# Ring tiles of 768 instead of 770 columns, and a first block whose convolution reads no history

## The chip, the cores and the metric

The kernel runs on one core of one Trainium2 chip. The metric is device time in microseconds, the median of several executions; before the change it was 2507.09 us in three (2506.99 to 2508.43).

## What is computed

One layer of a hybrid model is applied to 2048 prompt tokens and to 64 tokens of a sample that continues an earlier sequence. All arithmetic is float32; the widths are 1024 (model), 8 heads of 128 (path B) and 256 (side input).

```python
proj = rms_norm(x, g_pre) @ w_in                 # 1024 -> 10 x 1024
vA, bA, cA, zA, q, f, iv, zB, gA, gB = split(proj)
u = cA * vA
u_ext = concat([conv_hist, u])                   # two tokens of history; zeros for the prompt
conv = w[0] * u_ext[0:T] + w[1] * u_ext[1:T+1] + w[2] * u_ext[2:T+2]
yA = (silu(zA) * bA * conv) @ w_a_out
new_conv = u_ext[-2:]
# path B: gated recurrence over chunks of 64 tokens, o normalised per head
yB = (o * silu(zB)) @ w_b_out
out = (sigmoid(gA) * yA + sigmoid(gB) * yB) @ w_o
x = x + rms_norm(out, g_post)
x = x + (p @ w_ple_proj) * sigmoid(rms_norm(x, g_ple) @ w_ple_gate)
```

The outputs are x for prompt and sample, the last two columns of u for both, and the final states of path B for both.

## The kernel before

Everything is held with features on the 128 partitions and tokens along the columns. The 2112 tokens stand in one row (1408 of the prompt, the 64 of the sample, the other 640 of the prompt) and are cut into three blocks of 768, 704 and 640 columns, done one after the other. Within a block a matrix product takes halves of 384, 352 or 320 columns as its moving operand.

A float32 product is made of three matmuls in a reduced format: each operand is split into a high part (a copy by ACT) and the remainder (a subtraction by DVE, both in `split`, L230), and TensorE (PE) adds hi by hi, hi by lo and lo by hi into the same PSUM bank. In `sgroup` (L457 to L459), `in_turn` (L608 to L610) and `mm3` (L645 to L647) these three are the innermost lines. `sgroup` and `in_turn` do a 2x2 block product with seven instead of eight partial products, from sums of weight blocks and sums of operand halves. The plain products of the side input are L1313 to L1315.

Weights come by DMA in tiles of 128x512, issued by SyncE's queue, into a pool of their own (`raw`, `hi`, `lo`, `s`). Almost everything else on chip lies in one ring of 48 tiles: operands, activations, gates, intermediate rows. `rt()` (L155) hands out the next tile of that ring, `[P, BN + 2]` float32, of which callers use the first 768, 704 or 640 columns. BN is 768; the two extra columns are there for one use, the convolution's u, which needs two columns of history ahead of each run of tokens.

In SBUF each tile is given a multiple of 32 bytes per partition. The weight tiles of 2048 bytes all start at a multiple of 64. A ring tile of 770 columns is 3080 bytes and takes 3104; the ring starts at byte 70080, which is a multiple of 64.

The order of instructions on an engine is the order in which the program is written, with priorities (`tc.high_priority`) and places (`issue_after`, `hooks`) that put side work between the matmuls. DVE, ACT and POOL each run their rows in order; POOL also issues the DMAs of ring tiles, SyncE those of weights.

The change touches `path_a`, the stage of each block after path B, which runs over eight column groups j. For each j: POOL copies two columns of history ahead of each run of tokens in u (L899: from `hist_p` for the prompt, from `hist_s` for the sample); `sgroup` makes vA and cA, whose product DVE writes into u behind the history (`times_u`, L906); ACT multiplies u by the first tap into `conv` (L923), DVE adds the two others (L925, twice), and POOL copies u's last two columns back into the history (L926). Then zA and bA are made and multiplied in. `hist_p` is set to zero at the start (L195); block 0 has a single run, all of the prompt. Blocks 1 and 2 have two runs and one.

Of the kernel before, what the change touches and what calls it, by code (L numbers as in the profile page):

```python
# [14 lines left out]
ALU = mybir.AluOpType  # L15
# [3 lines left out]
P = 128  # L19
# [18 lines left out]
BN = max(SIZES)  # L38
# [56 lines left out]
def hybrid_step(  # L95
# [17 lines left out]
    V, A, G, T, SP = nc.vector, nc.scalar, nc.gpsimd, nc.tensor, nc.sync  # L113
# [5 lines left out]
    ring = ctx.enter_context(tc.tile_pool(name="ring", bufs=RING))  # L119
# [7 lines left out]
    def nm(s):  # L127
        uid[0] += 1
        return f"{s}_{uid[0]}"
# [22 lines left out]
    def hn():  # L152
        return width[0] // 2

    def rt(n=0, dt=F32):  # L155
        t = ring.tile([P, BN + 2], dt, tag="r", name=nm("r"))
        return t if n is None else t[:, : n or width[0]]

    def hf(n=0):
# [24 lines left out]
    cw = [vec[:, 4 + i, :] for i in range(3)]  # L184
# [7 lines left out]
    lb, omlb, nomlb, tmp = (lbt[:, i, :] for i in range(4))  # L192
    lb0, lb1 = vec[:, 7, :], vec[:, 8, :]
    hist_p = const.tile([P, KB, 2], F32, tag="histp", name="hist_p")
    V.memset(hist_p, 0.0)  # L195
    hist_s = const.tile([P, KB, 2], F32, tag="hists", name="hist_s")
    states = [None] * NH

    def constants():
        for rows, base in ((slice(0, CH), 0), (slice(CH, P), CH)):  # L200
            tri = rt(P)
            G.memset(tri, 1.0)
            G.affine_select(
                out=tri, in_=tri, pattern=[[1, P]], compare_op=ALU.is_ge, fill=0.0, base=base, channel_multiplier=-1
            )
            swapped = tri[rows, CH:] if base else tri[rows, :CH]
            V.tensor_copy(caus[rows], tri[rows, :CH])
            V.tensor_copy(caus2[rows, :SWAP, :], swapped.unsqueeze(1).to_broadcast([CH, SWAP, CH]))
            if base == 0:
                V.tensor_copy(caus2[:, SWAP:, :], tri[:, CH:].unsqueeze(1).to_broadcast([P, SWAP, CH]))  # L210
        V.memset(keep, 1.0)
        V.memset(keep.rearrange("p (c t) -> p c t", t=CH)[:, :, 0:1], 0.0)
        for t in atts:
            V.memset(t, 0.0)
# [17 lines left out]
    def split_rt(src):  # L232
        hi, lo = rt(dt=F32R), rt(dt=F32R)
        split(src, hi, lo)
        return hi, lo
# [139 lines left out]
    def prepare_sums(firsts, shared=False, pieces=False):  # L375
# [7 lines left out]
        def tile_of(dt=F32):  # L383
            return rt(4 * P, dt).rearrange("p (k c) -> p k c", c=P)
# [105 lines left out]
    def half(t, h):  # L490
        return t[:, h * hn() : (h + 1) * hn()]

    def whole(x, y):

        if y is None:
            return x
        t = hf()
        freed[:] = [V.tensor_tensor(t, x, y, ALU.add).ins]
        return t

    def into(dst, x, y):
        if y is None:
            A.copy(dst, x)
        else:
            V.tensor_tensor(dst, x, y, ALU.add)  # L505
# [384 lines left out]
    def path_a(bl, hc, a, first, extra, ready):  # L890

        for j in range(KB):
            next(extra, None)
            n = bl["n"]
            pos = [r[0] + 2 * i for i, r in enumerate(bl["runs"])]
            hists = [hist_s if r[2] else hist_p for r in bl["runs"]]
            ct, u, conv = rt(), rt(None), rt()
            for q, hist in zip(pos, hists):
                G.tensor_copy(u[:, q : q + 2], hist[:, j, :])  # L899
            left = {}  # L900

            def times_u(h, v):
                for (o, ln, _), q in zip(bl["runs"], pos):
                    lo, hi = max(o, h * hn()), min(o + ln, (h + 1) * hn())
                    if lo < hi:
                        V.tensor_tensor(  # L906
                            u[:, q + 2 + lo - o : q + 2 + hi - o], v[:, lo - h * hn() : hi - h * hn()], ct[:, lo:hi], ALU.mult
                        )

            def sink_u(c, h, x, y):  # L910
                if c == 1:
                    into(half(ct, h), x, y)
                    if h == 0:
                        times_u(0, left["v"])
                elif h == 0:
                    left["v"] = x
                else:
                    times_u(1, whole(x, y))

            sgroup(VA * 8 + j, CA * 8 + j, hc, sink_u, first)  # L920
            for (o, ln, _), q, hist in zip(bl["runs"], pos, hists):
                d = conv[:, o : o + ln]
                A.mul(d, u[:, q : q + ln], cw[0][:, j : j + 1])  # L923
                for w in (1, 2):
                    V.scalar_tensor_tensor(d, u[:, q + w : q + w + ln], cw[w][:, j : j + 1], d, ALU.mult, ALU.add)  # L925
                G.tensor_copy(hist[:, j, :], u[:, q + ln : q + ln + 2])  # L926
            z, b = rt(), rt()

            def sink_z(c, h, x, y):
                if c == 1:  # L930
                    into(half(b, h), x, y)
                else:
                    A.activation(half(z, h), whole(x, y), AF.Silu)

            if j == KB - 1:
                ready()
            sgroup(ZA * 8 + j, BA * 8 + j, hc, sink_z, first)
            V.tensor_tensor(conv, conv, b, ALU.mult)
            V.tensor_tensor(conv, conv, z, ALU.mult)
            a.append(conv)  # L940
# [669 lines left out]
    for n in range(4):  # L1610
# [5 lines left out]
        with behind_all(done):  # L1616
            for i in range(3 * n, 3 * n + 3):
                t, total = rows[i], ss[:, i % 2, i // 2 : i // 2 + 1]
# [53 lines left out]
    for bi, bl in enumerate(blocks):  # L1672
        first, kept = bi == 0, kepts[bi]
# [22 lines left out]
        def ready():  # L1696
            a_first.extend(narrow(half(t, 0)) for t in a[:KH])

        fresh[:] = ("S1", "S2") if bl["last"] else ()
        path_a(bl, hc, a, first, side(rows), ready)  # L1700
        fresh.clear()
        assert not hooks
# [133 lines left out]
```

## Time and profile before

| | |
|---|---|
| runs | 2506.99, 2507.09, 2508.43 us |
| profiled execution, first to last instruction | 2509.2 us |
| matmuls | 16254, granted clock 0.999 |
| DMA | 746.14 MB, 297 GB/s on average |
| SyncE's queue (q1) | 60.3% of 16 engines' span |
| POOL's queue (q0) | 25.1% |
| stage of the change in block 0 | about 437 to 665 us |

How to read it: a row of a group names line, engine, operation, output and inputs by the program's names (buffer numbers left out), then the count, busy time in us, mean ns of one, and the engine's idle time just before them with what ended it. In the timeline a row has its start in us and its duration. Matmuls are pipelined and their durations are modelled, so that one starts well before the other's end; the time that PE takes for one is the distance from its start to the next one's. The waits say who waited for whom, in us in total, times, and the longest.

### The profile page before, as it was taken

How to read it: one execution, taken by the hardware profiler on the slowest of the kernel's cores; microseconds unless marked ns; L12 is line 12 of the kernel's file. 1: busy time of each engine (PE TensorE's matmuls, PEld its weight loads, DVE VectorE, ACT ScalarE, POOL GpSimd, SP SyncE). 2: the span in 40 equal slices, each digit the busy share in tenths (PEclk: the TensorE clock that was granted, in tenths of full speed). 3: DMA queues.
4: the chain of work that ended last, by engine and by line, in shares of the span. 5: the costliest groups of instructions: out<-in, count | busy, mean ns of one | idle time of the engine just before them, and what ended most of it. 6: DMA issues, size and time to landing. Idle time of an engine off the chain costs nothing.

```text
span 2509.2 us, 47311 instructions
## 1 busy us (share of the span) xinstructions
PE 2491.1 (99%) x16254; PEld 2474.0 (99%) x16254; DVE 1932.2 (77%) x3699; ACT 1503.9 (60%) x2926; POOL 513.9 (20%) x875
## 2 busy tenths in 40 slices
PE   9999999999999999999999999999999999999998
PEld 9999999999999999999999999999999999999998
DVE  7889999988868775588886657977677776678766
ACT  6676676554453664466655556576666655565646
POOL 2032223321022021122223211102122222111031
PEclk9999999999999999999999999999999999999999
DMA  8789888997697798788889988979988879889887
GB/s 330 241 302 336 320 297 318 331 321 271 229 339 259 250 329 295 258 270 287 283 278 332 337 293 307 327 266 357 349 284 289 278 257 313 297 274 337 294 302 259
DMA packets 344240, 746.14 MB, mean 297 GB/s; under 512 B 43318, under 2 KB 48496, under 8 KB 344000
## 3 DMA queue, kind: packets, MB, share of 16 engines
q1 hardware_dynamic: 287136, 519.96, 60.3%
q0 software_dynamic: 56864, 223.16, 25.1%
q8 instruction: 128, 2.10, 0.3%
q14 instruction: 112, 0.92, 0.1%
HBM read 530.59 MB, written 212.36 MB: 296 GB/s over the span
## 4 chain that ended last, share of the span: by engine, by line
PE 90%; DMA 3%; DVE 3%; ACT 2%; issue 1%; POOL 0%; SPq 0%; ACTq 0%; DVEq 0%; POOLq 0%
PE pg L457 20%; PE pg L458 19%; PE pg L459 19%; PE pg L609 5%; PE pg L608 5%; PE pg L610 5%; PE pg L646 3%; PE pg L647 3%; PE pg L645 3%; DMA raw<-S 2%; PE pa L1142 1%; PE pa L1110 1%; PE pa L1180 1%; PE pa L1182 1%; DMA raw<-w_blk 1%
## 5 line engine op out<-in xcount | busy, mean ns | idle before, releaser
L457 PE MATMUL pg<-r,hi 128*128 128x320 f32 (+2 forms) x3304 | 1074.7, 325 | 1.1 <-DVE r L505 1.1
L458 PE MATMUL pg<-r,hi 128*128 128x320 f32 (+2 forms) x3304 | 1066.8, 323 | 0.0
L459 PE MATMUL pg<-r,lo 128*128 128x384 f32 (+2 forms) x2380 | 775.3, 326 | 0.4 <-DMA lo<-low 0.4
L457 PEld LDWEIGHTS pg<-r,hi 128*128 128x128 f32 x3304 | 621.0, 188 | 3.5 <-DVE r L505 1.7
L458 PEld LDWEIGHTS pg<-r,hi 128*128 128x128 f32 x3304 | 621.6, 188 | 0.0
L279 ACT CAST hi<-raw 128x512 fp32r<-128x512 f32 x566 | 349.9, 620 | 415.4 <-PE pg L458 170.6
L459 PEld LDWEIGHTS pg<-r,lo 128*128 128x128 f32 x2380 | 447.1, 188 | 0.7 <-DMA lo<-low 0.7
L230 ACT CAST hi<-raw 128x512 fp32r<-128x512 f32 x404 | 249.5, 621 | 206.3 <-PE pg L458 83.8
L609 PE MATMUL pg<-r,hi 128*128 128x320 f32 (+2 forms) x976 | 312.1, 321 | 2.5 <-DVE r L230 2.5
L608 PE MATMUL pg<-r,hi 128*128 128x320 f32 (+2 forms) x976 | 309.8, 320 | 0.0
L459 PE MATMUL pg<-r,s 128*128 128x352 f32 (+1 forms) x924 | 291.4, 315 | 0.0
L230 DVE TENSOR_TENSOR lo<-raw,hi 128x512 fp32r<-128x512 f32 x304 | 208.1, 686 | 82.7 <-ACT hi L230 75.9
L230 DVE TENSOR_TENSOR r<-r,r 128x320 fp32r<-128x320 f32 (+7 forms) x374 | 220.2, 608 | 46.1 <-ACT r L230 44.9
L230 ACT CAST r<-r 128x320 fp32r<-128x320 f32 (+7 forms) x374 | 195.9, 557 | 35.0 <-DVE r L1353 9.0
L610 PE MATMUL pg<-r,lo 128*128 128x320 f32 (+2 forms) x640 | 204.2, 319 | 0.1
L609 PEld LDWEIGHTS pg<-r,hi 128*128 128x128 f32 x976 | 183.2, 188 | 4.6 <-DVE r L230 4.3
L608 PEld LDWEIGHTS pg<-r,hi 128*128 128x128 f32 x976 | 182.3, 188 | 1.4 <-ACT r L230 1.0
L230 ACT CAST hi<-s 128x512 fp32r<-128x512 f32 x164 | 101.9, 623 | 127.3 <-PE pg L458 97.0
L459 PEld LDWEIGHTS pg<-r,s 128*128 128x128 f32 x924 | 173.5, 188 | 0.0
L471 ACT COPY hf<-pg 128x352 f32<-128x352 f32 (+2 forms) x354 | 157.5, 448 | 0.8 <-PE pg L459 0.7
L230 DVE TENSOR_TENSOR lo<-s,hi 128x512 fp32r<-128x512 f32 x164 | 114.2, 696 | 45.6 <-ACT hi L230 43.1
L505 DVE TENSOR_TENSOR r<-hf,pg 128x128 f32<-128x128 f32 (+5 forms) x164 | 64.3, 411 | 98.7 <-PE pg L459 98.6
(389 smaller groups left out, 4223.4 us busy)
## 6 DMA issues: line engine op xcount, KB each, us to landing
raw<-w_blk SPq DMA_DIRECT2D x559, 256.0 KB, 4.6
raw<-S SPq DMA_DIRECT2D x452, 256.0 KB, 4.2
lo<-low SPq DMA_DIRECT2D x340, 256.0 KB, 4.4
s<-low SPq DMA_DIRECT2D x226, 256.0 KB, 5.1
low<-lo SPq DMA_DIRECT2D x207, 256.0 KB, 3.9
S<-s SPq DMA_DIRECT2D x152, 256.0 KB, 4.2
low<-r POOLq DMA_DIRECT2D x66, 256.0 KB, 4.5
r<-w_blk POOLq DMA_DIRECT2D x64, 256.0 KB, 6.7
```

Of the source, the lines that this page charges most:

```text
L230: return A.copy(hi, src).ins, V.tensor_tensor(lo, src, hi.bitcast(F32), ALU.subtract).ins
L279: A.copy(hi, raw)
L457: add(hi[:, k, :], xhi, start=start and k == 0, stop=False)
L458: add(hi[:, k, :], xlo, start=False, stop=False)
L459: last[0] = add(lo[:, k, :], xhi, start=False, stop=k == KH - 1).ins
L471: copied = A.copy(got[n], ps[bank])
L608: add(hi[:, k, :], xhi, start=start and k == 0, stop=False)
L609: add(hi[:, k, :], xlo, start=False, stop=False)
L610: last[0] = add(lo[:, k, :], xhi, start=False, stop=k == KH - 1).ins
L645: T.matmul(ps, hi[:, k % 4, :], xhi[:, c], start=k == ks[0], stop=False)
L646: T.matmul(ps, hi[:, k % 4, :], xlo[:, c], start=False, stop=False)
L647: last[0] = T.matmul(ps, lo[:, k % 4, :], xhi[:, c], start=False, stop=k == ks[-1]).ins
```

## The change

The ring's tile is `[P, BN]`, 768 columns. In SBUF a tile then takes 3072 bytes, 48 x 64, so that all 48 start at multiples of 64 bytes; before, they were 3104 bytes apart, and every other tile started at 32 bytes beyond a multiple of 64. The u of block 1 has 704 columns and two runs, 708 with history, and that of block 2 640 and one run, 642: both fit. That of block 0 has 768 and one run, and would need 770. So in block 0 (`first`) u is stored without history, from column 0 on. The taps are applied in the other direction: the third tap (`cw[2]`) to all columns by ACT, then the second from the second column on, 767 columns, and the first from the third on, 766, by DVE. What the zero history would have added is left out. The memset of `hist_p` and block 0's eight copies out of it are gone; the copies back into it stay.

```diff
     def rt(n=0, dt=F32):
-        t = ring.tile([P, BN + 2], dt, tag="r", name=nm("r"))
+        t = ring.tile([P, BN], dt, tag="r", name=nm("r"))
         return t if n is None else t[:, : n or width[0]]
...
     hist_p = const.tile([P, KB, 2], F32, tag="histp", name="hist_p")
-    V.memset(hist_p, 0.0)
...
-            pos = [r[0] + 2 * i for i, r in enumerate(bl["runs"])]
+            pos = [r[0] + 2 * i - 2 * first for i, r in enumerate(bl["runs"])]
             hists = [hist_s if r[2] else hist_p for r in bl["runs"]]
             ct, u, conv = rt(), rt(None), rt()
-            for q, hist in zip(pos, hists):
-                G.tensor_copy(u[:, q : q + 2], hist[:, j, :])
+            if not first:
+                for q, hist in zip(pos, hists):
+                    G.tensor_copy(u[:, q : q + 2], hist[:, j, :])
...
                 d = conv[:, o : o + ln]
-                A.mul(d, u[:, q : q + ln], cw[0][:, j : j + 1])
-                for w in (1, 2):
-                    V.scalar_tensor_tensor(d, u[:, q + w : q + w + ln], cw[w][:, j : j + 1], d, ALU.mult, ALU.add)
+                A.mul(d, u[:, q + 2 * first : q + 2 * first + ln], cw[2 * first][:, j : j + 1])
+                for w in (1, 0) if first else (1, 2):
+                    at = (2 - w) * first
+                    V.scalar_tensor_tensor(
+                        d[:, at:], u[:, q + w + at : q + w + ln], cw[w][:, j : j + 1], d[:, at:], ALU.mult, ALU.add
+                    )
                 G.tensor_copy(hist[:, j, :], u[:, q + ln : q + ln + 2])
```

In the new kernel, lines between the memset and `path_a` are one lower and lines behind `path_a` three higher; its L926 is the DVE line that was L925, and its L929 the POOL line that was L926. Two places show what stands on the engines. The first is DVE in block 0, first column group of `path_a`, before the change: the two additions of the convolution (L925, into the tile r_5707) stand among state updates of path B (L1157) and splits of weights (L230, into a `lo` tile).

```order
L1157 SCALAR_TENSOR_TENSOR r_5914<-r_5914,qc_5281,pa_5909 128x128
L925 SCALAR_TENSOR_TENSOR r_5707<-r_5706,vec,r_5707 128x768
L1157 SCALAR_TENSOR_TENSOR r_5914<-r_5914,qc_5281,pa_5909 128x128
L230 TENSOR_TENSOR lo_5974<-raw_5929,hi_5973 128x512
L1157 SCALAR_TENSOR_TENSOR r_5914<-r_5914,qc_5281,pa_5909 128x128
L925 SCALAR_TENSOR_TENSOR r_5707<-r_5706,vec,r_5707 128x768
```

And after it, the same place on DVE, with the tiles' numbers one or two lower:

```order
L1160 SCALAR_TENSOR_TENSOR r_5912<-r_5912,qc_5280,pa_5907 128x128
L926 SCALAR_TENSOR_TENSOR r_5706<-r_5705,vec,r_5706 128x767
L1160 SCALAR_TENSOR_TENSOR r_5912<-r_5912,qc_5280,pa_5907 128x128
L229 TENSOR_TENSOR lo_5972<-raw_5927,hi_5971 128x512
L1160 SCALAR_TENSOR_TENSOR r_5912<-r_5912,qc_5280,pa_5907 128x128
L926 SCALAR_TENSOR_TENSOR r_5706<-r_5705,vec,r_5706 128x766
```

Only the two sizes differ. The second place is POOL in block 0, second column group, before the change: the copy out of the history (L899, into u's tile r_6146) ahead of stores of prepared weight sums (L398, L404) and of a turn through memory for path B (L1067, L1072), and the copy back (L926).

```order
L702 TENSOR_TENSOR ms_6114<-ms_6114,mhalf 128x2
L899 COPY r_6146<-hist_p 128x2
L398 DMA low_6262<-r_6263 128x512
L398 DMA low_6267<-r_6268 128x512
L404 DMA S_1571_6437<-r_6059 128x512
L1067 DMA to_6287<-r_5283 128x768
L1072 DMA r_6086<-to_6287 128x4x192
L926 COPY hist_p<-r_6146 128x2
```

And after it, the same place on POOL, where L397 and L403 are the stores and L929 the copy back:

```order
L701 TENSOR_TENSOR ms_6112<-ms_6112,mhalf 128x2
L397 DMA low_6259<-r_6260 128x512
L397 DMA low_6264<-r_6265 128x512
L403 DMA S_1571_6434<-r_6057 128x512
L1070 DMA to_6284<-r_5282 128x768
L1075 DMA r_6084<-to_6284 128x4x192
L929 COPY hist_p<-r_6144 128x2
```

The copy out of the history is gone and the rest stands as it did. PE's rows, 15143 of them, are the same before and after but for lines and numbers, and so are the semaphores that it waits for. On ACT two rows, on DVE four and on SyncE one change places with a neighbour or move by up to three rows, all in or just behind this stage of block 0.

## The prediction, made before the changed kernel was run

> **What bounds the kernel now.** First the page: busy time, then the chain of work that ended last.
>
> ```profile
> PE 2491.1 (99%) x16254; PEld 2474.0 (99%) x16254; DVE 1932.2 (77%) x3699; ACT 1503.9 (60%) x2926; POOL 513.9 (20%) x875
> ...
> PE 90%; DMA 3%; DVE 3%; ACT 2%; issue 1%; POOL 0%; SPq 0%; ACTq 0%; DVEq 0%; POOLq 0%
> PE pg L457 20%; PE pg L458 19%; PE pg L459 19%; PE pg L609 5%; PE pg L608 5%; PE pg L610 5%; PE pg L646 3%; PE pg L647 3%; PE pg L645 3%; DMA raw<-S 2%; PE pa L1142 1%; PE pa L1110 1%; PE pa L1180 1%; PE pa L1182 1%; DMA raw<-w_blk 1%
> ```
>
> PE is busy for 99% of the span and carries 90% of the chain, nearly all of it in the three matmuls of a product (hi by hi, hi by lo, lo by hi). Then the waits of PE, longest in total first: microseconds, times, longest.
>
> ```profile
> PE pg L609 <- DVE r L230: 2.5, 4, 0.9
> PE pa L722 <- DVE r L742: 1.3, 1, 1.3
> ...
> PE pg L459 <- DMA lo<-low: 0.4, 1, 0.4
> PE pa L1142 <- POOL r L1078: 0.4, 1, 0.4
> ```
>
> No entry is over 2.5 us, and the one wait for a DMA is 0.4 us. So no other engine and no transfer can give back more than a few microseconds; what can is the distance between one matmul's start and the next. It is read from the timeline, in one stretch for each width (start, modelled duration; ends of runs without a gap).
>
> ```profile
> 499.73 0.34 PE L457 MATMUL pg<-r,hi 128*128 128x384 f32 x1
> ...
> 502.19 0.34 PE L459 MATMUL pg<-r,lo 128*128 128x384 f32 x1
> ...
> 1399.78 0.32 PE L457 MATMUL pg<-r,hi 128*128 128x352 f32 x1
> ...
> 1401.86 0.33 PE L458 MATMUL pg<-r,hi 128*128 128x352 f32 x1
> ...
> 2149.86 0.31 PE L457 MATMUL pg<-r,hi 128*128 128x320 f32 x1
> ...
> 2151.93 0.31 PE L459 MATMUL pg<-r,lo 128*128 128x320 f32 x1
> ```
>
> 384 columns: 14 steps in 2.46 us, 175.7 ns each. 352: 13 in 2.08 us, 160.0. 320: 14 in 2.07 us, 147.9. The modelled durations of the groups overlap, but grow by the same step, 14 ns for 32 columns:
>
> ```profile
> L458 PE MATMUL pg<-r,hi 128*128 128x352 f32 x1120 | 361.8, 323 | 0.0
> ...
> L458 PE MATMUL pg<-r,hi 128*128 128x384 f32 x1064 | 358.5, 337 | 0.0
> ...
> L458 PE MATMUL pg<-r,hi 128*128 128x320 f32 x1120 | 346.5, 309 | 0.0
> ```
>
> Of PE's 16254 matmuls 14568 are of these three widths, and their distances add up to 2371 us, from the 320 columns' 4800 to the 384 columns' 4920 back to back. A change that leaves their order alone moves the end by whatever it does to the distance, and by little else.
>
> **The change, part by part.** *Positions of the ring tiles.* A tile of 770 columns is 3080 bytes and is rounded up to 3104, so from byte 70080 the even slots start at a multiple of 64 and the odd ones 32 bytes beyond one. A tile of 768 columns is 3072 bytes: all 48 slots start at multiples of 64, and so do second halves (320, 352 or 384 columns on, 1280, 1408 or 1536 bytes). Whether that is worth anything to PE can be asked of the old trace, since half of its ring tiles are at each kind of place. I took the starts of all 14568 matmuls between these two rows, gave each the address of its moving operand, and split the distances to the next start.
>
> ```profile
> 5.84 0.67 PE L1313 MATMUL pa<-r,r 128*128 128x384 f32 x1
> ...
> 2502.05 0.30 PE L610 MATMUL pg<-r,lo 128*128 128x320 f32 x1
> ```
>
> Without the 244 distances that are some 11 ns or more above their width's usual one, where PE waited, the means at 0 and at 32 beyond a multiple of 64 are 146.29 and 147.00 ns for 320 columns, 160.71 and 160.97 for 352, 174.70 and 175.15 for 384. The sign is the same at all three widths. The counts at 32 beyond are 2436, 2232 and 2570, so the plain split is worth 2436 x 0.71 + 2232 x 0.26 + 2570 x 0.45 = 3.5 us. With the stretch of 50 us and the line of the code held equal the difference is 0.42 ns; 7238 x 0.42 = 3.0 us. I take the 3.0, since slot and use of a tile go together. How sure is it? Over the 187 different addresses the means scatter by 1.3 ns, so the difference of two halves of them is uncertain by 1.3 x 2 / sqrt(187) = 0.19 ns: 0.42 +- 0.19, or 1.6 to 4.4 us.
>
> There is a reason that would make it real. The means over both kinds, 146.7, 160.8 and 174.9 ns, rise by 0.442 ns a column. The Trainium skill (TensorE: Matmul & The Clock Gate, section on the 56 ns) puts a warm matmul at N / 2.4 GHz plus 2.5 ns: by it 384 columns would take an estimated 162.5 ns, which this trace does not bear out (174.9), and nothing would depend on the place. Against its 0.417 ns a column, the 0.442 are an estimated one clock more for each 16 columns, which is 64 bytes; an operand that starts 32 beyond a multiple of 64 touches one more such piece, one clock. That agrees with the 0.42 measured, which does not need it.
>
> *The other engines.* Does DVE or ACT mind where an operand lies? The convolution reads one ring tile 4 and 8 bytes off (L925), the scalings of L805 and L1453 do not; the splits of L230 run on weight tiles, all at multiples of 64, and on ring tiles.
>
> ```profile
> L230 DVE TENSOR_TENSOR lo<-raw,hi 128x512 fp32r<-128x512 f32 x304 | 208.1, 686 | 82.7 <-ACT hi L230 75.9 <-DMA raw<-w_blk 3.8 <-PE pa L1110 1.8
> ...
> L230 DVE TENSOR_TENSOR r<-r,r 128x512 fp32r<-128x512 f32 x66 | 44.8, 683 | 2.6 <-ACT r L230 2.6
> ...
> L230 ACT CAST r<-r 128x512 fp32r<-128x512 f32 x66 | 40.4, 619 | 5.4 <-DVE r L401 5.4
> ...
> L925 DVE SCALAR_TENSOR_TENSOR r<-r,vec,r 128x768 f32<-128x768 f32 x16 | 16.2, 1013 | 2.9 <-ACT r L923 2.9
> ...
> L805 DVE SCALAR_TENSOR_TENSOR r<-r,vec,r 128x768 f32<-128x768 f32 x8 | 7.9, 1012 | 0.1
> L1453 DVE SCALAR_TENSOR_TENSOR r<-r,vec,r 128x768 f32<-128x768 f32 x8 | 7.9, 1011 | 0.4 <-ACT r L733 0.4
> ```
>
> 1013 against 1012 and 1011 ns, 686 against 683: they don't. The new forms of 767 and 766 columns, written 4 and 8 bytes into the tile, cost what L925 costs now, within a few nanoseconds, sixteen times. Transfers into ring tiles may land a little earlier or later; PE's only wait for a transfer is the 0.4 us above, so I put that at nothing. If that cover failed, what is late next would be a weight tile, not a ring tile.
>
> *The first block's convolution.* It loses eight POOL copies of two columns (L899), the memset of the history (one DVE instruction ahead of all work), and nothing else. The stage lies at 437 to 665 us.
>
> ```profile
> L899 POOL COPY r<-hist_p x24: 183/262/1461, 437.5 to 2191.0; 128x2 f32<-128x2 f32 x24
> ...
> its engine sat idle before it (us, times) until:
> who waited for it (us, times):
> ```
>
> That is the copy's own line: shortest, median and longest in ns, and two lists that are empty. POOL did not wait ahead of it, and nobody waited for it. What POOL does wait for in this step is the copy back into the history, which stays:
>
> ```profile
> POOL hist_p L926 <- DVE r L906: 213.8, 24, 28.8
> ```
>
> And the stage in stretches: length, then busy time of PE, its weight loads, DVE, ACT and POOL, with granted clock, DMA share and GB/s at the end.
>
> ```profile
> 400.00:450.00 50.00, 50.00 (x327) 49.68 (x326) 47.84 (x90) 34.97 (x72) 14.54 (x21) 1.00 0.87 306
> 450.00:500.00 50.00, 50.00 (x300) 50.00 (x299) 47.09 (x85) 29.28 (x68) 16.32 (x29) 1.00 0.94 330
> ...
> 550.00:600.00 50.00, 50.00 (x288) 49.91 (x288) 44.60 (x78) 25.89 (x53) 9.41 (x17) 1.00 0.82 281
> 600.00:665.00 65.00, 65.00 (x373) 65.00 (x372) 52.11 (x85) 27.89 (x51) 2.99 (x7) 1.00 0.71 238
> ```
>
> PE has work in every microsecond of it, and POOL is busy for 16 of 50 us at most. Eight medians of 262 ns are 2.1 us of POOL time that nobody is short of. With the copy gone, the first to write into a slot of the ring is DVE's product L906, which would now wait for the slot; queued behind it on DVE are splits of weights, for which PE waits. But the copy did not idle before it, so the slot was free by then: nothing. A few POOL, ACT, DVE and SP instructions change places by one to three rows in this stage. DVE, at 47 of 50 us, is the one that could be late; PE's order and its waits are the same as before. Between nothing and one wait of the size of the largest above, 1.3 us, either way; I take nothing, by the row of 50.00 in 50.00.
>
> **The sum.** -3.0 us for the positions, 0 for the rest. The profiled execution spans 2509.2 us from first to last instruction, the runs take 2506.99 to 2508.43; the change is the same in both, so 2507.1 - 3.0 = 2504.1 us. What a measurement of this kernel can tell from no change I take as 0.2%, 5.0 us.
>
> **The rivals.**
>
> *The place does not matter* (2507.1 us). The split compares tiles that also do different things, and 0.42 is only 2.2 times its uncertainty. By the Trainium skill (SBUF — State Buffer, section on the DMA port swizzle) a line of this memory has 16 bytes; 0 and 32 beyond a multiple of 64 both begin one, and by that rule the change is worth nothing. Against it: three widths of one sign. Within 0.2% too.
>
> *The place matters more, in steps of 256 bytes* (2502.0 us or less). Split by eight places in 256 bytes, with the width's mean taken off, 3842 matmuls at 32 and 64 beyond a multiple of 256 are dear, +1.37 +- 0.26 and +0.52 +- 0.31 ns, and the other 10433 are -0.35. All first halves now start 192 beyond. If that is as good as the others, 14568 x 0.35 = 5.1 us go; if it is one uncertainty better than measured there (-0.18 - 0.30), 7.0 us, 2500.1 us. Against it: at 192 itself I measured -0.18, and second halves of 352 columns come to 64 beyond, a dear place; 5/6 x 0.18 - 1/6 x 0.52 leaves 0.06 ns, 0.9 us, 2506.2 us.
>
> *Slower: all operands of PE start at the same place* (2511.6 us at its upper end). Weight tiles start 448 beyond a multiple of 512. Now all first halves do too, and second halves of 384 columns: some 9700 matmuls, against 828 before. Those 828 are +0.17 +- 0.30 ns dearer than the rest. At +0.17 that is 1.6 us, at +0.47 it is 4.5 us and 2511.6 us if nothing is gained; from 0.52 ns on it passes 0.2%. The next load of weights and the running product would have to get into each other's way for that; PE's loads are busy 2474.0 us beside 2491.1 of products, so they do run side by side.
>
> *The reordered rows of the first block make PE wait* (2507.1 +- 1.3 us, or with the forecast's gain 2502.8 to 2505.4 us): a DVE split one row late. PE has no idle time there.
>
> **How the numbers follow.** The forecast 0.42; the place does not matter 0.27; steps of 256 bytes 0.15; the same place 0.10, of which 0.07 beyond 0.2%; the reordered rows 0.06. Faster by over 0.2% (below 2502.1) is the third case alone, 0.15; slower (above 2512.1) 0.07; within, 0.78. The range goes from 2500.5, which takes in most of the third case, to 2510.0, which takes in the second and half of the fourth.
>
> **What would show it.** In the profile after, the same count of matmuls in the same order, and start-to-start distances near 146.3, 160.7 and 174.7 ns at all tiles: stretches of 384 columns at 174.7, not 175.7, and the last matmul some 3 us earlier against the first. The waits of PE keep the same entries, none new from L906 or its convolution. The forecast is wrong if the distances stay at 146.7, 160.8 and 174.9, or if PE gains an entry over 2 us in the stage at 437 to 665 us.

## The result, and the profile after

The changed kernel takes 2493.86 us (median of five, 2493.57 to 2495.75), the kernel before beside it 2506.99 (five, 2505.62 to 2508.43): ratio 0.9949, 95% interval 0.9938 to 0.9960. That is 13.1 us less. Forecast were 3.0 us less; the range began at 2500.5. The direction was right, the size four times too small.

The page after, busy time and chain (line numbers are those of the new kernel; L456 to L458 are the three matmuls of `sgroup`):

```profile
PE 2476.7 (99%) x16254; PEld 2460.1 (99%) x16254; DVE 1930.7 (77%) x3698; ACT 1501.9 (60%) x2926; POOL 514.4 (21%) x867
...
PE 91%; DVE 4%; DMA 2%; issue 2%; ACT 1%; POOL 0%; DVEq 0%; ACTq 0%; POOLq 0%
```

PE's busy time is 14.4 us less for the same 16254 matmuls, that of its weight loads (PEld) 13.9 us less; those of DVE, ACT and POOL are within 2.0 us of what they were. Now PE's waits, longest in total first.

```profile
PE pa L1316 <- ACT r L1323: 1.3, 1, 1.3
PE pg L456 <- DVE r L504: 1.2, 1, 1.2
...
PE pg L458 <- DMA lo<-low: 0.4, 1, 0.4
```

They were small and are small; none is for the convolution. So no wait went away that could hold 13 us: the matmuls themselves follow each other faster. The three stretches of the timeline, at the same places of the program:

```profile
495.25 0.33 PE L456 MATMUL pg<-r,hi 128*128 128x384 f32 x1
...
497.68 0.33 PE L458 MATMUL pg<-r,lo 128*128 128x384 f32 x1
...
1388.67 0.32 PE L456 MATMUL pg<-r,hi 128*128 128x352 f32 x1
...
1390.75 0.32 PE L457 MATMUL pg<-r,hi 128*128 128x352 f32 x1
...
2135.99 0.31 PE L456 MATMUL pg<-r,hi 128*128 128x320 f32 x1
...
2138.04 0.31 PE L458 MATMUL pg<-r,lo 128*128 128x320 f32 x1
```

384 columns: 14 steps in 2.43 us, 173.6 ns (175.7 before). 352: 13 in 2.08 us, 160.0 (160.0 before too, in a stretch that lay below that width's old mean of 160.83). 320: 14 in 2.05 us, 146.4 (147.9). The groups say it over many more, in the second matmul of the three, as modelled durations:

```profile
L457 PE MATMUL pg<-r,hi 128*128 128x352 f32 x1120 | 360.6, 322 | 0.0
L457 PE MATMUL pg<-r,hi 128*128 128x384 f32 x1064 | 355.8, 334 | 0.0
...
L457 PE MATMUL pg<-r,hi 128*128 128x320 f32 x1120 | 346.3, 309 | 0.0
```

337 became 334 at 384 columns, 323 became 322 at 352, 309 stayed at 320. Measured over all 14568 matmuls as in the prediction (starts, without the distances where PE waited), start to start in ns, with the scatter of single distances in brackets:

| | 320 columns | 352 | 384 |
|---|---|---|---|
| before | 146.64 (2.45) | 160.83 (2.64) | 174.95 (2.40) |
| after | 146.64 (0.83) | 159.71 (2.48) | 173.40 (0.89) |

1.55 ns x some 4900 is 7.6 us, 1.12 x some 4850 is 5.4 us: 13.0 us, as much as the medians lost. The two profiled executions lie further apart, 17.3 us (spans of 2509.2 and 2491.9 us): the distances where PE waited sum up to some 4 us less after, most of it at 320 columns, and whether that belongs to the change is not shown. The table shows too that the scatter is no measure of the gain: at 320 columns it fell and the mean stayed, at 352 the mean fell and the scatter stayed. Why the distances fell is what the runs were for.

### The profile page after: what moved, and what is told of

Its sections match the earlier page's. It is cut to its first block, busy times and chain, and to the rows that moved or that the text cites. A ratio compares the mean times of both kernels' runs of the same rounds, so it can differ in the third digit from the quotient of the medians.

```text
span 2491.9 us, 47297 instructions
## 1 busy us (share of the span) xinstructions
PE 2476.7 (99%) x16254; PEld 2460.1 (99%) x16254; DVE 1930.7 (77%) x3698; ACT 1501.9 (60%) x2926; POOL 514.4 (21%) x867
## 4 chain that ended last, share of the span: by engine, by line
PE 91%; DVE 4%; DMA 2%; issue 2%; ACT 1%; POOL 0%; DVEq 0%; ACTq 0%; POOLq 0%
PE pg L456 20%; PE pg L457 20%; PE pg L458 19%; PE pg L608 6%; PE pg L607 6%; PE pg L609 6%; PE pg L645 3%; PE pg L646 3%; PE pg L644 3%; PE pa L1145 1%; PE pa L1113 1%; PE pa L1183 1%; PE pa L1185 1%; DMA raw<-S 1%; PE pa L1316 0%
## 5 line engine op out<-in xcount | busy, mean ns | idle before, releaser
L456 PE MATMUL pg<-r,hi 128*128 128x320 f32 (+2 forms) x3304 | 1071.8, 324 | 1.4 <-DVE r L504 1.2
L458 PE MATMUL pg<-r,lo 128*128 128x384 f32 (+2 forms) x2380 | 771.1, 324 | 0.9 <-DVE lo L229 0.5
L456 PEld LDWEIGHTS pg<-r,hi 128*128 128x128 f32 x3304 | 620.8, 188 | 3.7 <-DVE r L504 1.9
L458 PEld LDWEIGHTS pg<-r,lo 128*128 128x128 f32 x2380 | 447.0, 188 | 1.5 <-DVE lo L229 0.8
L458 PE MATMUL pg<-r,s 128*128 128x352 f32 (+1 forms) x924 | 291.6, 316 | 0.0
L458 PEld LDWEIGHTS pg<-r,s 128*128 128x128 f32 x924 | 173.6, 188 | 0.0
```

The lines of the kernel that those rows point to most:

```text
L456: add(hi[:, k, :], xhi, start=start and k == 0, stop=False)
L458: last[0] = add(lo[:, k, :], xhi, start=False, stop=k == KH - 1).ins
```

## The experiments

The place of an operand means here its start address modulo 256 bytes. The expectations name theories by letters:

- A: what matters is that operands start at multiples of 64 bytes.
- B: what matters is that all of them have one common place.
- C: the gain comes from the edits of the convolution.
- D: TensorE's own reads set the distance. D1 says that the places alone do, D2 that the place itself counts beside the difference of two places.
- S: the accesses of the other engines to the same memory set it.
- H: what the matmuls came from (the way in) counts too.
- W: the place of the moving operands against that of the weights counts.

Each whole kernel ran beside the kernel before, which took 2507.6 to 2508.0 us in the median, and its ratio is to that; the runs of matmul patterns were executed once each. Means of distances are taken from the starts in the traces, as in the table above.

**Which part of the change.** The first two kernels are the kernel after with longer ring tiles: 3104 bytes apart again (e2), and 3136 apart, all at multiples of 64 but at four places of 256 (e3, with fewer buffers for two small tiles to make room).

```diff
-        t = ring.tile([P, BN], dt, tag="r", name=nm("r"))
+        t = ring.tile([P, BN + 8], dt, tag="r", name=nm("r"))     # BN + 16 in e3
```

> The new kernel with ring tiles of 776 columns, 3104 bytes apart as before: the positions are undone, the convolution without history stays. Theories A and B: 2507 us, distances of before (175.0, 160.8 and 146.6 ns). Theory C: 2494 us.

> The new kernel with ring tiles of 784 columns, 3136 bytes apart: all tiles at multiples of 64 bytes, but at four places in 256 bytes (two small pools have fewer buffers to make room). Theory A: 2494 us. Theory B: the places differ as they did before, if in steps of 64 bytes: nearer 2507 than 2494 us, and distances of 384 columns that scatter as before. Theory C: 2494 us.

e2 took 2509.49 us, ratio 1.0007 [0.9998, 1.0016]: the convolution's edits bring no gain, theory C is out. e3 took 2505.88, 0.9992 [0.9982, 1.0001]. Multiples of 64 alone are worth 3.6 us against e2, or 2.1 us against the kernel before with an interval that takes in zero. That is near the forecast, and not the 13. Its distances are 146.47, 160.81 and 174.94 ns, close to those of before.

The next two keep all ring tiles at one common place, 32 bytes beyond a multiple of 64: in e1 the ring moves alone, in e4 the ring and the weights' pool ahead of it.

```diff
+    ring.tile([P, 8], F32, tag="pad", name="pad", bufs=1)     # e1, ahead of the ring's tiles
+    const.tile([P, 8], F32, tag="pad", name="pad")            # e4, ahead of both pools
```

> The new kernel with 32 bytes of unused memory ahead of the ring, so that all 48 ring tiles start 32 bytes beyond a multiple of 64, and all at the same place in 256 bytes (224). Theory A, multiples of 64 are what counts (half of the tiles off cost 13 us, so all of them off cost about twice that): near 2520 us, PE's start-to-start distance 1.8 ns over the new kernel's. Theory B, what counts is that all moving operands start at one and the same place, whichever it is: 2494 us, distances as in the new kernel (173.4 ns at 384 columns, 159.7 at 352, 146.6 at 320). Theory C, the gain is from the first block's convolution and the copies that went: 2494 us, with the distances of before where a tile is off.

> The new kernel with 32 bytes of unused memory ahead of weights and ring, so that both start 32 bytes beyond a multiple of 64 and keep their places against each other. Theory A: 2520 us, or more if weights count too. Theory B: 2494 us. If only the place of the moving operand against the weights counts, this one is at 2494 us where the ring alone shifted is not.

e4 took 2496.53 us, 0.9956 [0.9941, 0.9971], e1 2499.09, 0.9965 [0.9952, 0.9977]. No operand was at a multiple of 64 and most of the gain stayed: A is out. e4's distances are those of after (173.36 ns at 384), e1's a little longer (173.61, 352 columns 160.03 for 159.71). The intervals of the two times overlap, so the times do not tell them apart; the distances do, and between e1 and e4 only the place of the weights differs. That was the first sign of W.

**PE's reads, or the others'?** Both next kernels run only matmuls in patterns of 120, three per product as in the kernel, with operands at chosen distances; in the second DVE and ACT work beside them on tiles at mixed places. Here and in the two grids further on, operands and weights start at the same place of 256 bytes where nothing else is said.

> Only products, no model: it leaves out the whole computation, so only its trace is read. Thirty patterns of 120 matmuls each on PE with nothing else running, operands 3072, 3072 (all 32 bytes off), 3104, 3136, 3200 and 3328 bytes apart, for 384, 352 and 320 columns, then two places in turn. Theory D, PE's own reads set the distance (one common place is cheap, mixed places dear): 3072 and 3072+32 bytes at 173.4 ns for 384 columns, 3104 and 3136 near 175.0; no difference for 320 columns. Theory S, the other engines' accesses to mixed places take PE's time: the same distance in every pattern of one width, since nothing else runs.

> The same products, while DVE and ACT work through tiles at mixed places all the time (the computation is left out again). Theory D: the distances of the kernel without the side work, pattern by pattern. Theory S: distances longer than there, by up to 1.6 ns at 384 columns.

Both leave out the computation, so only their distances are read. Alone, lines L57 (tiles 3072 bytes apart), L59 (3104), L62 (3328, 13 x 256), L69 (320 columns, 3072 apart) and L83 (320 columns, low operands 32 bytes beyond the high ones). Columns: shortest, median, longest modelled ns; first and last start in us.

```profile
L57 PE MATMUL pg<-big,w x120: 334/334/335, 57.1 to 77.7; 128*128 128x384 f32 x120
...
L59 PE MATMUL pg<-big,w x120: 331/337/343, 98.7 to 119.5; 128*128 128x384 f32 x120
...
L62 PE MATMUL pg<-big,w x120: 333/334/337, 161.8 to 182.4; 128*128 128x384 f32 x120
...
L69 PE MATMUL pg<-big,w x120: 303/309/312, 298.3 to 315.7; 128*128 128x320 f32 x120
...
L83 PE MATMUL pg<-big,w x120: 302/308/310, 565.2 to 582.4; 128*128 128x320 f32 x120
```

First to last start over 119 steps, from the unrounded starts: 173.33 ns at a common place, 174.73 at 3104, 175.55 at 3136, and 173.35 again at 3328. So PE by itself, with no other engine at work, shows both the kernel's 175 and its 173.4. Tiles 3328 bytes apart, a multiple of 256, are as cheap as one place, tiles 3136 apart, a multiple of 64, are not: what counts is the place in 256 bytes, not in 64 or 16. At 320 columns the common place gives 146.64 and 32 bytes between high and low 144.48. Beside DVE and ACT:

```profile
PE 592.5 (58%) x3672; PEld 591.9 (58%) x3672; DVE 901.9 (88%) x1301; ACT 970.2 (95%) x1523; POOL 0.2 (0%) x4
```

```profile
L59 PE MATMUL pg<-big,w x120: 331/337/343, 98.7 to 119.5; 128*128 128x384 f32 x120
```

Pattern by pattern the distances are the same to 0.01 ns. The shares of the page are of a span that runs on after the matmuls; from 57 to 592 us, under the patterns, DVE and ACT were each busy for 95% of the time, and the granted clock was 1.00. Theory S is out, D stands. The Trainium skill (SBUF — State Buffer, section on the DMA port swizzle) has lines of 16 bytes in this memory. All these places begin one; by that rule alone the patterns would be equal, and they are 2.2 ns apart (175.55 and 173.33); the measurement decides.

In the kernel the same is asked by mixing the places again in blocks 1 and 2 (0 to 224 bytes in turn), of PE's operands alone (e5, `dt == F32R`) or of all other ring tiles (e6, `dt == F32`):

```diff
-        return t if n is None else t[:, : n or width[0]]
+        if n is None:
+            return t
+        n, o = n or width[0], 0
+        if dt == F32R and width[0] < BN and n <= width[0]:
+            turns[0] += 1
+            o = 8 * (turns[0] % 8)
+        return t[:, o : o + n]
```

> The new kernel; in blocks 1 and 2 (704 and 640 columns) the tiles that hold split operands of PE start 0 to 224 bytes into their ring tile, in turn, so that the moving operands are at mixed places, and all else is where it was. Theory D: 160.8 ns instead of 159.7 at 352 columns, 146.6 as before at 320, 173.4 at 384 (block 0, untouched), some 5 us slower than the new kernel, 2499 us. Theory S: 159.7 ns and 2494 us, or little over.

> The opposite: in blocks 1 and 2 all ring tiles but the split operands start 0 to 224 bytes into their ring tile, in turn; the moving operands stay at common places. Theory D: 159.7 ns at 352 columns, 2494 us. Theory S: 160.8 ns and about 2499 us.

e5: 2500.95 us, 0.9971 [0.9961, 0.9981]; 352 columns back at 160.90 ns, 384, which it leaves alone, at 173.40. e6: 2496.11, 0.9949 [0.9934, 0.9964], all three distances as after. In modelled durations, the second matmul of the three at 352 columns, e5 and then e6 (361.8 before, 360.6 after):

```profile
L463 PE MATMUL pg<-r,hi 128*128 128x352 f32 x1120 | 361.6, 323 | 0.0
```

```profile
L463 PE MATMUL pg<-r,hi 128*128 128x352 f32 x1120 | 360.5, 322 | 0.0
```

That is theory D.

**What rule do PE's reads follow?** Patterns again, first a grid of places for high and low operand.

> TensorE's products alone, as in the last measurement; everything else is left out, so the outputs are not the reference's. For 320, 352 and 384 columns, all 64 pairs of places of the high and the low operand in 256 bytes (steps of 32 bytes), 60 products each; then low operands 4 to 80 bytes beyond the high ones at 320 columns; then the weights moved by 0 to 224 bytes, the operands left where they are. Theory D1 (only the difference of the two places counts): every pattern of one difference has one distance: at 320 columns 146.65 ns at 0, 144.45 at 32 and 64 bytes, 146.55 at 128; at 384 columns 173.33 at 0 and 175.6 at 32; at 352 columns 160.0 at 32. Theory D2 (the place itself counts too): patterns of one difference lie over 0.5 ns apart, as at 352 columns with one common place, where 160.03 and 161.05 ns stood for two places. Weights: if only the moving operand counts, the eight distances of moved weights agree within 0.1 ns; if the weights' place counts against the operand's, they spread by 1 ns or more.

There is no rule of the difference alone: at 384 columns the patterns of one and the same difference (0) run from 173.3 to 176.7 ns, so D1 in its simple form fell, and D2 holds. With the operands left in place, moving the weights alone spreads them from 173.3 to 176.6. What orders them is, for the most part, the place of the operands (both at one place) against that of the weights. The same quantity was swept twice, by moving the operands or by moving the weights the other way: 384 columns, ns, over the last 42 of each pattern's distances:

| operands beyond weights, bytes | 0 | 32 | 64 | 96 | 128 | 160 | 192 | 224 |
|---|---|---|---|---|---|---|---|---|
| operands moved | 173.33 | 173.33 | 173.33 | 176.64 | 176.14 | 173.33 | 176.67 | 173.33 |
| weights moved | 173.33 | 176.64 | 173.33 | 176.64 | 175.93 | 173.33 | 174.64 | 173.33 |

Six of the eight agree within 0.3 ns, two (32 and 192) do not. So the place against the weights is most of it and not all. The next run repeats eight patterns six times each, behind other patterns and behind pauses.

> Products alone again, all else left out, so the outputs are not the reference's. Eight patterns of 120 products, each six times: three times straight behind other patterns in shuffled order, three times behind a pause of TensorE of one, two or three VectorE copies. Patterns: 384 columns with one common place, the same with the weights 160 bytes further, the same with both operands 32 bytes further, and with the low operands 32 bytes beyond the high ones; 320 columns with one common place, with the low ones 32 bytes further, and that with the weights 128 bytes further; 352 columns with one common place. Theory D1 (the places alone set the distance): a pattern's six means agree within 0.2 ns, and differ between patterns: 173.3 ns for the common place, 144.5 for 320 columns with 32 bytes between, over 174.5 for 384 with 32 bytes between. Theory H (the products settle into one of several repeating orders, and which one depends on how they came in): the six means of a pattern lie on two or more values, 0.5 ns or more apart, in above half of the patterns; the common place may then merely have more ways that end at 173.3.

384 columns: L68 and L80 are the common place of operands and weights, L67 and L88 weights 160 bytes further, L70 and L104 low operands 32 bytes beyond the high ones. First to last start is 119 steps: 20.6, 21.0 or 21.1, and 20.9 against 20.7 us.

```profile
L68 PE MATMUL pg<-big,w x120: 334/334/337, 125.6 to 146.2; 128*128 128x384 f32 x120
...
L80 PE MATMUL pg<-big,w x120: 334/334/337, 357.0 to 377.6; 128*128 128x384 f32 x120
...
L67 PE MATMUL pg<-big,w x120: 337/338/343, 104.4 to 125.4; 128*128 128x384 f32 x120
...
L88 PE MATMUL pg<-big,w x120: 337/338/343, 512.8 to 533.9; 128*128 128x384 f32 x120
...
L70 PE MATMUL pg<-big,w x120: 334/337/341, 165.7 to 186.6; 128*128 128x384 f32 x120
...
L104 PE MATMUL pg<-big,w x120: 331/336/421, 677.3 to 698.0; 128*128 128x384 f32 x120
```

Means of the second half of each pattern, ns, six repeats:

| pattern | values (times) |
|---|---|
| 384, operands at the weights' place | 173.3 (6) |
| 384, weights 160 further (operands 96 beyond) | 176.7 (6) |
| 384, operands 32 beyond | 173.3 (5), 176.7 (1) |
| 384, low ones 32 beyond the high | 175.6 (4), 173.3 (2) |
| 352, at the weights' place | 161.1 (4), 160.0 (2) |
| 320, at the weights' place | 146.7 (6) |
| 320, low ones 32 beyond | 144.4 (2), 145.6 (4) |
| 320, the same, weights 128 further | 146.7 (4), 148.2 (2) |

Each repeat settles into a short cycle of distances that repeats but for a nanosecond or two (173, 173, 174; or 175, 177, 175, 180). Five of eight patterns have two such cycles, and the way in chooses: H. But the common place has one at 384 columns and at 320. At 384 columns the means lie up to 3.3 ns apart, at 320 up to 3.8, and the weights' place moves them. If that is so in the kernel, mixing the weights' places must take the gain back though the operands keep one common place (e7; its longer weight tiles move the ring as a whole, to 32 in 256 bytes), and moving all operands together to a bad place against the weights must make it slower than before (e9, 96 bytes).

```diff
+    def wt(tag, dt=F32R, **kw):
+        return wp.tile([P, 520], dt, tag=tag, name=nm(tag), **kw)[:, :512].rearrange("p (k c) -> p k c", c=P)
...
-        hi = wp.tile([P, 4, P], F32R, tag="hi", name=nm("hi"))
+        hi = wt("hi")
```

The tiles `lo` and `s` come from `wt` in the same way. And e9, as e1 with another size:

```diff
+    ring.tile([P, 24], F32, tag="pad", name="pad", bufs=1)
```

> The kernel after, with the tiles of high and low weights 2080 bytes apart in place of 2048, so that weights start at eight places of 256 bytes; all moving operands keep one common place. Theory D in the form 'the moving operands alone set the distance': 2494 us (2491 to 2497), 384 columns at 173.4 ns, 352 at 159.7, 320 at 146.65. Theory W (place of the moving operand against that of the weights that are loaded beside it): as the eight places of weights averaged in the grid, 174.7 ns at 384 columns and 146.7 at 320, so 1.2 ns x 4900 = 6 us more: 2500 us (2497 to 2505).

> The kernel after with one tile of 96 bytes ahead of the ring, so that all moving operands still have one common place, but the weights lie 160 bytes beyond it in 256 instead of at it. Theory D (the moving operands' common place suffices): 2494 us (2491 to 2497), 384 columns at 173.4 ns. Theory W (their place against that of the weights decides, each pairing having its own distances): at 384 columns the six repeats with weights 160 bytes further gave 176.6 ns, so 3.2 ns x 4900 = 16 us more in the first block, about 2510 us in all, slower than the kernel before if the two other widths stay as they are; those were not measured at this place and may add or take 1 ns x 9600, so 2500 to 2520 us.

e7 took 2507.26 us, ratio 0.9998 [0.9989, 1.0008]: the whole gain is gone, more than either theory gave. The page and the second matmul at 384 columns:

```profile
PE 2490.2 (99%) x16254; PEld 2473.3 (99%) x16254; DVE 1930.8 (77%) x3698; ACT 1503.3 (60%) x2926; POOL 510.8 (20%) x867
...
L460 PE MATMUL pg<-r,hi 128*128 128x384 f32 x1064 | 357.5, 336 | 0.0
```

Distances 146.70, 160.85 and 174.81 ns: those of before, to 0.15. At 384 columns the eight places of the sweep average 174.5 with operands moved and 174.6 with weights moved. What the expectation missed was 352 columns, which it left out: 1.14 ns x 4850 is 5.5 us. e7's trace also shows that the price is not one of the pair alone: 889 matmuls of 384 columns have operand and weights at one place, but stand among others, and they take 175.66 ns where all together took 173.40. e9 took 2517.31 us, ratio 1.0036 [1.0022, 1.0051], slower than the kernel before by 9.6 us. Its page and the stretch of 384 columns at the same place of the program:

```profile
PE 2500.3 (99%) x16254; PEld 2483.3 (99%) x16254; DVE 1933.1 (77%) x3698; ACT 1504.6 (60%) x2926; POOL 513.2 (20%) x867
...
L458 PE MATMUL pg<-r,hi 128*128 128x384 f32 x1064 | 360.2, 339 | 0.0
```

```profile
502.57 0.34 PE L457 MATMUL pg<-r,hi 128*128 128x384 f32 x1
...
505.05 0.34 PE L459 MATMUL pg<-r,lo 128*128 128x384 f32 x1
```

14 steps in 2.48 us are 177.1 ns; over all of them 176.59, where the repeats had 176.7. Against after that is 3.19 x 4900 = 15.6 us, and 352 columns at 161.49 add 1.78 x 4850 = 8.6: 24.2 us, of 23.5 measured. So one common place of the operands does not suffice: B is out, and so is D in the form that the moving operands alone decide. One stretch of the same trace is a control: the first 96 matmuls of 384 columns have their weights in the ring too, so at the operands' place, and take 173.60 ns (173.68 after), the others 176.64. W stands for 384 columns, in the kernel as alone. At 352 it stands in part. There the second halves lie 128 bytes beyond the weights after the change, and their distance fell more than that of the first halves (161.07 to 159.32 ns, against 160.63 to 160.05), some 3.8 of the 13 us; the pattern at that pairing alone took 162.24. So the patterns do not give that part. The weights start at 192 in 256 bytes, in before as in after; the ring begins at 192 too, and a stride of 3072, 12 x 256, puts every tile there. Nothing in the change asks for that: with a ring that began 96 bytes later it was a loss (e9).

**A faster one?** At 320 columns the low operands 32 bytes beyond the high ones were quicker alone. e8 does that in the last block, with `low()` in place of `rt(dt=F32R)` for low parts and the same shift in `narrow`'s second half:

```diff
+    def low():
+        o = 8 if width[0] == 640 else 0
+        return rt(None, F32R)[:, o : o + width[0]]
```

> The kernel after, with the low operands of the last block (640 columns, halves of 320) 32 bytes beyond the high ones. Theory D1 (the places alone): 144.5 ns in place of 146.65 over some 4700 distances: 10 us less, 2484 us (2481 to 2488). Theory H (the way in decides too): a mixture of 144.5, 146.65 and up to 149 ns, a mean of 145.8 to 147: 2490 to 2496 us.

2490.15 us (2487.74 to 2491.68), ratio 0.9929 [0.9913, 0.9945]; 320 columns at 144.89 ns. The second matmul of the three, and a stretch:

```profile
L461 PE MATMUL pg<-r,hi 128*128 128x320 f32 x1120 | 345.1, 308 | 0.0
```

```profile
2133.15 0.30 PE L460 MATMUL pg<-r,hi 128*128 128x320 f32 x1
...
2135.17 0.31 PE L462 MATMUL pg<-r,lo 128*128 128x320 f32 x1
```

14 steps in 2.02 us, 144.3 ns. That is D1's distance, nearly, but H's time: 1.75 x 4800 = 8.4 us less against after, of which 3.7 arrived in the medians. The distances 11 ns or more above their width's usual one, where PE waited, lie 28.2 us above it in sum, and 22.6 after: 5.6 of the 8.4 us went into waits, which leaves 2.8 (the profiled spans differ by 3.4). PE's waits in the profile add up to 11.2 us against 7.9, led by splits and sums on DVE:

```profile
PE pg L612 <- DVE r L233: 1.6, 3, 0.7
PE pg L460 <- DVE r L508: 1.5, 2, 0.9
```

The two intervals (0.9913 to 0.9945, 0.9938 to 0.9960) overlap a little, so the further 3.7 us against after are likely and not certain.

## Why the prediction was wrong

- *What bounds the kernel* was right: PE's distances carried the result, 13.0 of 13.1 us.
- *The first block's convolution and its reordered rows, 0 us:* right. e2 has both and takes 2509.49 us at a ratio of 1.0007.
- *The other engines, 0 us:* right. DVE went from 1932.2 to 1930.7 us, ACT from 1503.9 to 1501.9, and e6 and the patterns beside DVE and ACT show that their work did not change PE's distances.
- *Positions of the ring tiles, -3.0 us:* this is the step that failed. It split the old distances by each operand's own place, 0 or 32 beyond a multiple of 64, and took the difference as what a moved tile would gain. That takes the price of a matmul as a function of its own operand's address. It isn't: it belongs to the sequence, operands against one another and against the weights loaded beside them (e5, e7 and e9). In the old trace the places were mixed, so both halves of the split held mixed sequences and neither showed what a uniform one costs. The tiles that were at 0 already were forecast to stay at 174.70 and 160.71 ns; with all others the means went to 173.40 and 159.71. The term measured -13.1 us in place of -3.0, and e3, which makes only what the split spoke of, -3.6 against e2. That e3 came near the forecast does not save the term: the change puts nearly all operands at one place, and e3 does not. That this place is the weights' is luck: nothing in the change sets it, and the prediction named it as a danger only.
- *One clock for each 64 bytes* as the reason falls too. The 0.442 ns a column was a feature of mixed places: after, (173.40 - 146.64) / 64 is 0.418. On that the Trainium skill (TensorE: Matmul & The Clock Gate, section on the 56 ns) was right in the slope, N / 2.4 GHz; its 2.5 ns on top are 13.3 here at 384 columns, 173.33 - 160.0.
- *Rival in steps of 256 bytes:* right in the period and the sign, but it too summed places one by one and ended at 2500.1 us. The second halves of 352 columns, which it put at a dear place (64), became the cheapest of their width, 159.32 ns against 160.05.
- *Rival of one common place with the weights, slower:* it named the ingredient that decides, the load of weights beside the product, and had the sign wrong. Its 828 old matmuls at the weights' place were 0.17 ns dearer, in mixed company; with all 4920 of 384 columns at that place they are the cheap case, 173.40 ns. (By the addresses of the new program 10296 matmuls start 448 beyond a multiple of 512, not some 9700.) e9 shows the loss it feared, with the ring away from the weights.
- *What would show it:* 146.3, 160.7 and 174.7 ns were named, 146.64, 159.71 and 173.40 came. 352 and 384 columns fell by 1.12 and 1.55 ns where 0.1 and 0.25 were forecast, 320 by nothing where 0.35 was.

Open stays what in the chip makes the cycles: the runs show which places give which distance, not why. Open too is why the second halves of 352 columns, 128 bytes off the first, are cheaper in the kernel than in the patterns; no run moved them alone.

## What to carry to other kernels

Where PE is busy all the time, look at the start-to-start distances: 1.55 and 1.12 ns less at two widths were worth 13 us here, more than the 10.7 us of all of PE's waits in the profile before. For streams of such three-matmul products try moving operands and weights at one common place in 256 bytes (tile sizes in multiples of 256, pools begun alike), and measure: a common place 96 bytes away was worse than no order (e9), and at 320 columns another pairing was shorter still (e8). And a split of an old trace prices a change only if the trace holds stretches that look as the new program will; if every stretch is mixed, a small run of the uniform case is a better guide. Here it gave the price at 384 columns, and missed that of the second halves at 352.

## What the runs showed of the hardware

- The distance of matmuls varies with the places of moving operands and weights in 256 bytes, with no other engine at work: over the grid (m3) from 173.3 to 177.0 ns at 384 columns, 157.8 to 164.4 at 352 and 144.4 to 148.9 at 320, and up to 150.0 at 320 with tiles 3136 bytes apart (m1).
- Most steady means of the patterns stand on steps: 173.33, 174.43, 175.55, 176.67 ns at 384 columns, 160.0, 161.1 and 162.2 at 352, 144.43, 145.55, 146.67 at 320. At 384 columns a product of three matmuls so takes 520.0 ns in the mean, or once, twice or three times 3.33 ns more.
- With the same addresses two cycles are possible (175.6 and 173.3 ns), and what came before decides (m4). A pause of PE does not bring back one of them: behind pauses both occur.
- At the best, 320 columns took 144.4 ns, 2.2 ns less than at the common place; at 384 no pattern fell below 173.2.
- DVE and ACT, each busy for 95% of the time under the patterns, did not change one of 30 by more than 0.01 ns (m2 against m1).
